# Rotary exchange by DMA issued from ScalarE in the last heads, scaling on ScalarE, and another product order at the ends of the Strassen-like chains

## The chip, the cores and the metric

One Trainium2 chip, one core of it. The metric is the device time of one execution in microseconds; for the kernel before it is the median of three runs. All work is in fp32, and every product is made of three fp32r matmuls on a high and a low part of each operand (hi·hi, hi·lo, lo·hi).

## The reference, cut to what the change touches

One encoder layer over two groups of 512 tokens of width 1024 (prompt and sample), which share all weights. The change touches the rotary part of the queries, the softmax, and the products with w_mo, w_ao and the feed-forward weights:

```python
def rope(x, cos, sin):
    x1, x2 = jnp.split(x, 2, axis=-1)
    return jnp.concatenate([x1 * cos - x2 * sin, x1 * sin + x2 * cos], axis=-1)

# one head of attention (8 heads: 128 plain + 64 rotary query columns, values of 128)
s = q_nope @ k_nope.T + q_rope @ k_rope.T
p = jax.nn.softmax(s * scale, axis=-1)
o = p @ v
# both branches, merge, output, feed-forward
y_m = (sigmoid(o) * hm) @ w_mo
y_a = mla_attention(...) @ w_ao
x = x + (g_m * y_m + g_a * y_a) @ w_out
x = x + (silu(h2 @ w_gate) * (h2 @ w_up)) @ w_down
```

## The kernel before

The stages follow each other on one core: input projections, the mLSTM heads (to about 540 us), the eight attention heads (575 to 859), a first chain of products for w_mo and w_ao (859 to 1020), the output projection, a second chain for the feed-forward weights (about 1150 to 1776), the embedding gate and the last norm. Operands are kept transposed, with channels on the 128 partitions and 512 tokens along the row. Except where a block is pinned, a scheduler sets the order of each engine's instructions from a model of times, and each engine then runs its own list in order; a change of one instruction can so move others.

**Attention.** The loop at L1042 goes over heads `hd` and groups `g`: `attn(hd, g)` (L791) is followed by `attn_proj(hd + 1, g)` (L773), which prepares the next head, and by single steps (`hops`) that prepare the operands of the first chain, a few for each head. `attn_proj` makes the rotated queries in even heads for two heads at a time: the projection `pj` in PSUM, its product with the cosines (L744, `rp`), its product with the sines with neighbouring blocks of 32 rows exchanged (`rs`), and the sum of both (L755), all by `rope` (L741). In every head but head 0 the exchange is made by four multiplications of 32 rows each that write to other rows than they read (L754). In head 0 one multiplication of 128 rows writes `rm` (L748), and four transfers that SyncE issues bring its blocks to their places in `rs` (L752). ScalarE then casts the sum to the high parts `qs` (L778, L779) and VectorE makes the low ones (L780, L781). `attn` goes over four blocks of 128 queries: five matmuls of scores `sc` (L799 to L803), the maximum (L805, L806), the exponential (L808), the reciprocal of the sum (L809), the scaling of the probabilities by it, on ScalarE (L811) and for the block `i == 1` on VectorE (L813), four transposes into `pt` (L816), the high part on ScalarE (`aph`, L818) and the low part on VectorE (`apl`, L154). The value product `av` (L823 to L825) follows with all four blocks; `oz` (L827) is its copy, which goes to memory.

**Chains.** `chain` (L957) makes seven-product (Winograd) block multiplications. An object `Seven` (L904) is one set of four weight blocks, loaded by two transfers of 512 KB issued by ScalarE (L913, `wst`). `weights(name)` (L919) makes the weights of a product, by four adds of 128x512 per set on the engine `adds` (L927 and L928 for P7, L930 for P6, L937 for P3), and splits them (`wp`: L900 on ScalarE, L154 on VectorE). `product` (L941) issues twelve matmuls (L952 to L954) into a PSUM bank. P1 opens bank `b1`, and P6, P5 and P3 add to it; after P1, P6 and P5 ScalarE copies its contents to `u` (L987), so the next product in that bank waits for the copy. `chain` writes the order out:

```python
for n in ("P6", "+P1", "P5", "+P2", "Q4", "+P7", "P3"):   # "+": the next set's
```

The sets of the first chain are mo0 to mo3 and ao0 to ao3; those of the second are the feed-forward ones. `pair` (L1033) picks the engine of the adds in the first chain, VectorE (`V`) or GpSimd (`GP`).

Of the kernel before, what the change touches and what calls it, by code (L numbers as in the profile page):

```python
# [22 lines left out]
AH = 8  # L23
# [39 lines left out]
def encoder_kernel(ctx: ExitStack, tc: tile.TileContext, a):  # L63
    nc = tc.nc
# [324 lines left out]
    for g in range(G):  # L389
        s = EV("ch", "gsb")  # L390
# [349 lines left out]

    def rope(src, nblk, by_dma=False):  # L741
        n = 32 * nblk
        r = Q("tr", "rp")
        V.tensor_tensor(out=r[0:n], in0=src[0:n], in1=cos[0:n], op=ALU.mult)  # L744
        s = Q("tr", "rs")
        m = EV("ch", "rm") if by_dma else None
        if by_dma:
            V.tensor_tensor(out=m, in0=src, in1=sin, op=ALU.mult)  # L748
        for i in range(nblk):
            f, o = slice(32 * i, 32 * i + 32), slice(32 * (i ^ 1), 32 * (i ^ 1) + 32)  # L750
            if by_dma:
                nc.sync.dma_start(s[o], m[f])  # L752
            else:
                V.tensor_tensor(out=s[o], in0=src[f], in1=sin[f], op=ALU.mult)  # L754
        V.tensor_tensor(out=r[0:n], in0=r[0:n], in1=s[0:n], op=ALU.add)  # L755
        return r
# [16 lines left out]
    def attn_proj(hd, g, wa):  # L773
        if hd % 2 == 0:
            r = rope(proj1(wa, lat["cq"][g], 2, 0, "pj"), 4, hd == 0)
            st0 = Q("qst", "qs0", F32R)
# [14 lines left out]
    def attn(hd, g, ops):  # L791
# [4 lines left out]
        for i in range(NB):  # L796
# [12 lines left out]
            V.reciprocal(out=mx[:, 3:4], in_=mx[:, 2:3])  # L809
            if i != 1:  # L810
                S.activation(out=p, in_=p, func=AF.Copy, scale=mx[:, 3:4])  # L811
# [92 lines left out]
    class Seven:  # L904


        def __init__(self, srcs, kh, ops, out, adds=None):
# [8 lines left out]
            self.st, self.n, self.kh, self.ops, self.out = st, n, kh, ops, out  # L916
            self.bk = {}

# [22 lines left out]
        def product(self, name):  # L941
            whi, wlo = self.weights(name)
            b, first = {"P1": ("b1", 1), "P6": ("b1", 0), "P5": ("b1", 0), "P3": ("b1", 0), "P2": ("b0", 1),
# [13 lines left out]
    def chain(quads, head=False, look=4):  # L957

        order = [(0, n) for n in ("P1", "P2", "P7")]
        if head:  # L960
            order = [(0, "P1"), (0, "P2"), (1, "P1"), (1, "P2"), (0, "P7"), (0, "P6"), (0, "P5"), (0, "Q4"), (1, "P7"), (0, "P3")]
        for i in range(1 if head else 0, len(quads)):
            for n in ("P6", "+P1", "P5", "+P2", "Q4", "+P7", "P3"):
                if n[0] != "+":
# [68 lines left out]
    def pair(kind, c, ops, put):  # L1033
        e = V if kind == "mo" and c > 1 or kind == "ao" and c < 2 else GP
        srcs = [a["w8"][W8[f"{kind}{i}"]] for i in (c, c + 4)]
# [485 lines left out]
```

## Time and profile before

| what | value |
|---|---|
| median of three runs | 1883.64 us (1883.53 to 1885.17) |
| the profiled execution | 1885.68 us |
| its span in the trace | 1883.9 us |
| its mean granted TensorE clock | 0.993 |
| TensorE busy | 1844.1 us (98%) |
| VectorE busy | 1233.1 us (65%) |
| ScalarE busy | 884.5 us (47%) |
| GpSimd busy | 350.6 us (19%) |

PE is the matmuls of TensorE, PEld its weight loads, DVE VectorE, ACT ScalarE, POOL GpSimd, SP SyncE; a "q" behind an engine's name is its instruction queue, where transfers are issued. Matmuls overlap, so that one shows 0.39 us and the next starts sooner than that. The engines' shares are means over stages that differ much.

### The profile page before, as it was taken

What the parts mean: (1) busy time and instruction counts of PE and PEld (TensorE: products, weight loads), DVE (VectorE), ACT (ScalarE), POOL (GpSimd) and SP (SyncE); (2) the same over time, 40 slices, a digit from 0 to 9 for tenths busy, and PEclk for the clock granted to TensorE, in tenths of its full rate; (3) what the DMA queues carried; (4) which work ended last, traced back from release to release, by engine and by line L of the source; (5) the groups of instructions that cost most, each with busy time, mean ns of one, the idle gap of its engine ahead of it and who ended that gap; (6) DMA issues with size and microseconds to landing.
All of it is one profiled execution on the core that took longest, in us unless ns stands there. A gap on an engine that the chain in (4) does not pass through costs nothing.

```text
span 1883.9 us, 24465 instructions
## 1 busy us (share of the span) xinstructions
PE 1844.1 (98%) x8849; PEld 1534.2 (81%) x8849; DVE 1233.1 (65%) x2208; ACT 884.5 (47%) x1726; POOL 350.6 (19%) x273
## 2 busy tenths in 40 slices
PE   9999999999999999899999999999999999999997
PEld 7899898988887888677877888888888877878886
DVE  7747575836554667975887487444444569878756
ACT  6255465534444666774534256333333344434433
POOL 0000000100000000250030002666466523111000
PEclk9999999999999999999999999999999999999998
DMA  4111111112254223445555342232323347533332
GB/s 166 52 45 35 57 34 58 40 60 73 79 176 135 65 73 95 125 150 196 164 193 174 101 151 79 95 129 92 103 91 106 119 144 240 159 129 109 99 133 95
DMA packets 98377, 208.11 MB, mean 110 GB/s; under 512 B 10832, under 2 KB 21456, under 8 KB 98256
## 3 DMA queue, kind: packets, MB, share of 16 engines
q1 hardware_dynamic: 85600, 161.72, 25.7%
q10 hardware_dynamic: 12096, 43.00, 7.0%
q8 instruction: 69, 1.13, 0.3%
q0 software_dynamic: 560, 1.84, 0.2%
q14 instruction: 52, 0.43, 0.1%
HBM read 151.89 MB, written 54.10 MB: 109 GB/s over the span
## 4 chain that ended last, share of the span: by engine, by line
PE 85%; DVE 9%; DMA 2%; ACT 2%; issue 1%; SPq 0%; ACTq 0%; DVEq 0%
PE b L952 13%; PE b L954 12%; PE b L953 12%; PE mm L183 8%; PE mm L185 8%; PE mm L184 8%; PE nm L633 3%; PE mm L79 3%; DVE xl L154 2%; PE mm L548 2%; PE mm L550 2%; PE mm L549 2%; PE pt L816 1%; PE mm L1312 1%; PE mm L1313 1%
## 5 line engine op out<-in xcount | busy, mean ns | idle before, releaser
L952 PE MATMUL b<-xh,wp 128*128 128x512 f32 x1148 | 441.8, 393 | 8.9 <-ACT u L987 3.7
L953 PE MATMUL b<-xl,wp 128*128 128x512 f32 x1148 | 448.2, 392 | 0.5 <-DVE xl L154 0.5
L954 PE MATMUL b<-xh,wp 128*128 128x512 f32 x1148 | 444.3, 392 | 0.7 <-DVE wp L154 0.7
L900 ACT CAST wp<-wst 128x512 fp32r<-128x512 f32 (+1 forms) x270 | 164.1, 612 | 306.8 <-PE b L954 256.6
L154 DVE TENSOR_TENSOR wp<-wst,wp 128x512 fp32r<-128x512 f32 (+1 forms) x270 | 233.1, 865 | 72.1 <-ACT wp L900 72.0
L952 PEld LDWEIGHTS b<-xh,wp 128*128 128x128 f32 x1148 | 215.8, 188 | 60.9 <-ACT u L987 7.6
L954 PEld LDWEIGHTS b<-xh,wp 128*128 128x128 f32 x1148 | 216.0, 188 | 48.6 <-DVE wp L154 1.6
L953 PEld LDWEIGHTS b<-xl,wp 128*128 128x128 f32 x1148 | 216.0, 188 | 48.0 <-DVE xl L154 1.4
L183 PE MATMUL mm<-hh,whi 128*128 128x512 f32 x560 | 220.3, 393 | 0.6 <-ACT raw L79 0.3
L184 PE MATMUL mm<-hl,whi 128*128 128x512 f32 x560 | 219.5, 392 | 0.0
L185 PE MATMUL mm<-hh,wlo 128*128 128x512 f32 x560 | 219.3, 392 | 0.0
L992 DVE TENSOR_TENSOR u<-b,u 128x512 f32<-128x512 f32 x90 | 61.6, 689 | 135.2 <-PE b L954 83.7
L183 PEld LDWEIGHTS mm<-hh,whi 128*128 128x128 f32 x560 | 105.6, 189 | 23.2 <-ACT raw L79 0.8
L168 ACT CAST whi<-wst 128x1024 fp32r<-128x1024 f32 (+1 forms) x69 | 71.0, 1029 | 113.7 <-PE mm L184 75.1
L185 PEld LDWEIGHTS mm<-hh,wlo 128*128 128x128 f32 x560 | 105.5, 188 | 21.9
L184 PEld LDWEIGHTS mm<-hl,whi 128*128 128x128 f32 x560 | 105.6, 189 | 21.4
L927 POOL TENSOR_TENSOR s<-wst,wst 128x512 f32<-128x512 f32 (+1 forms) x28 | 43.8, 1565 | 347.3 <-DMA wst<-w 175.1
L154 DVE TENSOR_TENSOR wlo<-wst,whi 128x1024 fp32r<-128x1024 f32 (+1 forms) x69 | 82.2, 1192 | 30.5 <-ACT whi L168 30.0
L987 ACT COPY u<-b 128x512 f32<-128x512 f32 x90 | 50.8, 589 | 108.9 <-PE b L954 85.7
L1210 POOL TENSOR_TENSOR sg<-sg,u 128x512 f32<-128x512 f32 x30 | 54.5, 1818 | 218.0 <-DVE u L992 218.0
L154 DVE TENSOR_TENSOR xl<-ld,xh 128x512 fp32r<-128x512 f32 x121 | 90.2, 773 | 7.2 <-ACT xh L884 6.5
L154 POOL TENSOR_TENSOR vnl<-avt,vnh 128x512 fp32r<-128x512 f32 x16 | 21.2, 1322 | 309.7 <-ACT vnh L158 251.3
(357 smaller groups left out, 3598.5 us busy)
## 6 DMA issues: line engine op xcount, KB each, us to landing
wst<-w SPq DMA_DIRECT2D x73, 512.0 KB
wst<-w ACTq DMA_DIRECT2D x60, 512.0 KB
ld<-actd SPq DMA_DIRECT2D x77, 256.0 KB
actd<-t SPq DMA_DIRECT2D x40, 256.0 KB
x<-x SPq DMA_DIRECT2D x32, 256.0 KB
ld<-hzd SPq DMA_DIRECT2D x32, 256.0 KB
wst<-wd ACTq DMA_DIRECT2D x16, 512.0 KB
actd<-sg SPq DMA_DIRECT2D x30, 256.0 KB
```

The costliest lines, as they stand in the source:

```text
L79: r = f(*args, **kw)
L154: e.tensor_tensor(out=out, in0=src, in1=hi.bitcast(F32), op=ALU.subtract)
L168: S.copy(hi[:, :n], st[:, :n])
L183: E.matmul(bk, whi[:, c], hi, start=k == 0, stop=False)
L184: E.matmul(bk, whi[:, c], lo, start=False, stop=False)
L185: last_mm[0] = E.matmul(bk, wlo[:, c], hi, start=False, stop=k == nk - 1)
L633: E.matmul(bk, l, r, start=n == 0, stop=n == len(terms) - 1)
L900: S.copy(hi, src)
L952: E.matmul(bk, whi[:, c], hi, start=bool(first) and k == 0, stop=False, **sk)
L953: E.matmul(bk, whi[:, c], lo, start=False, stop=False, **sk)
L954: E.matmul(bk, wlo[:, c], hi, start=False, stop=k == self.kh - 1, **sk)
L992: V.tensor_tensor(out=t, in0=b, in1=t, op=ALU.add if name == "P2" else ALU.subtract)
```

## The change

Four edits:

1. In the heads 4 and 6 (two groups each, so four rotations) the exchange of rows goes as in head 0, but the transfers are issued by ScalarE (`S`).
2. The scaling of block `i == 1` goes from VectorE to ScalarE in heads 4, 5 and 6 (six instructions).
3. The last three sets of each chain get orders of their own, and the weights of P7 are made ahead of those of P6 where P7 follows P6.
4. In the first chain the adds of mo2 and ao1 go from VectorE to GpSimd.

```diff
-    def rope(src, nblk, by_dma=False):
+    def rope(src, nblk, by_dma=None):
...
             if by_dma:
-                nc.sync.dma_start(s[o], m[f])
+                by_dma.dma_start(s[o], m[f])
             else:
                 V.tensor_tensor(out=s[o], in0=src[f], in1=sin[f], op=ALU.mult)
...
-            r = rope(proj1(wa, lat["cq"][g], 2, 0, "pj"), 4, hd == 0)
+            r = rope(proj1(wa, lat["cq"][g], 2, 0, "pj"), 4, nc.sync if hd == 0 else S if hd >= 4 else None)
...
-            if i != 1:
+            if i != 1 or 4 <= hd < AH - 1:
                 S.activation(out=p, in_=p, func=AF.Copy, scale=mx[:, 3:4])
...
-            self.bk = {}
+            self.bk, self.w = {}, {}
...
         def product(self, name):
-            whi, wlo = self.weights(name)
+            if name == "P6" and "P7" not in self.w:
+                self.w["P7"] = self.weights("P7")
+            if name not in self.w:
+                self.w[name] = self.weights(name)
+            whi, wlo = self.w[name]
...
+        full = ("P6", "+P1", "P5", "+P2", "Q4", "+P7", "P3")
+        ends = {
+            len(quads) - 3: ("P6", "+P1", "P5", "+P2", "Q4", "P3"),
+            len(quads) - 2: ("P6", "P7", "P5", "+P1", "Q4", "P3"),
+            len(quads) - 1: ("P6", "P7", "P5", "P2", "Q4", "P3"),
+        }
         for i in range(1 if head else 0, len(quads)):
-            for n in ("P6", "+P1", "P5", "+P2", "Q4", "+P7", "P3"):
+            for n in ends.get(i, full):
...
-        e = V if kind == "mo" and c > 1 or kind == "ao" and c < 2 else GP
+        e = V if (kind, c) in (("mo", 3), ("ao", 0)) else GP
```

The scheduler moves other instructions with these. The number of matmuls stays. The three places below are those that matter for what follows; the names carry running numbers.

VectorE before, rotation of head 6, first group: `pj_7778` is the projection, `rp_7785` and `rs_7787` the two parts of the rotation, `pt` and `apl` the transposed probabilities of head 4, second group, and their low part, `xl` low parts of operands of the first chain.

```order
L744 TENSOR_TENSOR rp_7785<-pj_7778,cos 128x512
L754 TENSOR_TENSOR rs_7787<-pj_7778,sin 32x512
L154 TENSOR_TENSOR apl_7532<-pt_7566,aph_7531 128x4x128
L754 TENSOR_TENSOR rs_7787<-pj_7778,sin 32x512 x3
L805 TENSOR_REDUCE mx_7728<-sc_7722 128x1
L809 RECIPROCAL mx_7688<-mx_7688 128x1
L154 TENSOR_TENSOR xl_7839<-ld_7827,xh_7837 128x512
L154 TENSOR_TENSOR apl_7532<-pt_7586,aph_7531 128x4x128
L809 RECIPROCAL mx_7708<-mx_7708 128x1
L154 TENSOR_TENSOR xl_7845<-ld_7841,xh_7843 128x512
L755 TENSOR_TENSOR rp_7785<-rp_7785,rs_7787 128x512
```

VectorE with the change, the same rotation (`rp_7789`, `rs_7791`, and `rm_7792` before its exchange); `pt_7868` to `pt_7928` are the four blocks of head 5, second group.

```order
L748 TENSOR_TENSOR rm_7792<-pj_7782,sin 128x512
L154 TENSOR_TENSOR apl_7854<-pt_7868,aph_7853 128x4x128
L154 TENSOR_TENSOR xl_8304<-ld_8292,xh_8302 128x512
L154 TENSOR_TENSOR apl_7854<-pt_7888,aph_7853 128x4x128
L755 TENSOR_TENSOR rp_7789<-rp_7789,rs_7791 128x512
L154 TENSOR_TENSOR apl_7854<-pt_7908,aph_7853 128x4x128
L154 TENSOR_TENSOR apl_7854<-pt_7928,aph_7853 128x4x128
```

The rotation's product and its sum have moved back: the sum now stands between the low parts of the second and the third block of one value product. In the same place ScalarE has, with the change (`oz` the copy of the value product before, `vnh` and `qnh` casts of projections, `xh` a high part for the first chain):

```order
L818 CAST aph_7853<-pt_7868 128x4x128
L827 COPY oz_7779<-av_7766 128x512
L884 CAST xh_8302<-ld_8292 128x512
L818 CAST aph_7853<-pt_7888 128x4x128
L752 DMA rs_7791<-rm_7792 32x512 x4
L158 CAST vnh_7829<-avt_7827 128x512
L818 CAST aph_7853<-pt_7908 128x4x128
L818 CAST aph_7853<-pt_7928 128x4x128
L158 CAST qnh_7981<-pj_7974 128x512
L778 CAST qs_1320_7799<-rp_7789 64x512
L779 CAST qs_1321_7800<-rp_7789 64x512
```

The four issues stand behind the cast of the second block; the casts of the rotated rows (L778, L779) come after the last block's. What TensorE has between the transposes of the second and of the last block, ahead of the value product `av_7935`:

```order
L816 MATMUL pt_7888<-ident,p_7884 128x128 x4
L799 MATMUL sc_8070<-knh_7823,qnh_7812 128x512
L800 MATMUL sc_8070<-knl_7825,qnh_7812 128x512
L801 MATMUL sc_8070<-knh_7823,qnl_7814 128x512
L183 MATMUL pj_7974<-cqh_5518,whi_7680 128x512
L184 MATMUL pj_7974<-cql_5520,whi_7680 128x512
L185 MATMUL pj_7974<-cqh_5518,wlo_7682 128x512
L183 MATMUL pj_7974<-cqh_5522,whi_7680 128x512
L184 MATMUL pj_7974<-cql_5524,whi_7680 128x512
L185 MATMUL pj_7974<-cqh_5522,wlo_7682 128x512
L816 MATMUL pt_7908<-ident,p_7904 128x128 x4
L816 MATMUL pt_7928<-ident,p_7924 128x128 x4
```

Nine matmuls of 512 columns stand between the second block's transposes and the third's; the value product, which needs all four blocks, follows.

GpSimd before, adds of the first chain (`wst_8644` is of mo1, `wst_9544` and `wst_9546` are of ao2):

```order
L937 TENSOR_TENSOR wst_8644<-wst_8644 128x512
L927 TENSOR_TENSOR s_1743_9653<-wst_9544,wst_9546 128x512
L928 TENSOR_TENSOR wst_9546<-wst_9546 128x512
L930 TENSOR_TENSOR wst_9544<-wst_9544,wst_9546 128x512
L937 TENSOR_TENSOR wst_9544<-wst_9544 128x512
```

GpSimd with the change (`wst_8810` and `wst_8812` of mo2, `wst_9386` and `wst_9388` of ao1; `wst_8652` is mo1 as before):

```order
L937 TENSOR_TENSOR wst_8652<-wst_8652 128x512
L927 TENSOR_TENSOR s_1583_8913<-wst_8810,wst_8812 128x512
L928 TENSOR_TENSOR wst_8812<-wst_8812 128x512
L930 TENSOR_TENSOR wst_8810<-wst_8810,wst_8812 128x512
L937 TENSOR_TENSOR wst_8810<-wst_8810 128x512
L927 TENSOR_TENSOR s_1723_9511<-wst_9386,wst_9388 128x512
L928 TENSOR_TENSOR wst_9388<-wst_9388 128x512
L930 TENSOR_TENSOR wst_9386<-wst_9386,wst_9388 128x512
L937 TENSOR_TENSOR wst_9386<-wst_9386 128x512
L927 TENSOR_TENSOR s_1750_9683<-wst_9552,wst_9554 128x512
```

Eight adds have come in between those of mo1 and of ao2; they left VectorE's list. On TensorE the product of ao2 that opens its bank b1 stands 13 matmuls later in the first chain than before, and in the last set P5 and P3, which add to one bank, still follow each other.

## Rows read from the trace of the kernel before

**Rows 1.** The head of the page: the span, and each engine's busy time with its share of the span.

```profile
span 1883.9 us, 24465 instructions
PE 1844.1 (98%) x8849; PEld 1534.2 (81%) x8849; DVE 1233.1 (65%) x2208; ACT 884.5 (47%) x1726; POOL 350.6 (19%) x273
```

**Rows 2.** The waits of TensorE over the whole program: the waiting operation and its line, the one that ended the wait, total us, times, longest us.

```profile
PE sc L799 <- ACT p L808: 4.6, 5, 2.4
PE b L952 <- ACT u L987: 3.7, 9, 0.7
```

**Rows 3.** Busy time of each engine in stretches of the program: start:end and length in us, then busy us and (number of instructions) of PE, PEld, DVE, ACT and POOL, the granted clock of TensorE as a share of full speed, the busy share of the DMA engines, GB/s.

```profile
718.00:745.00 27.00, 27.00 (x132) 22.24 (x131) 23.73 (x51) 19.03 (x38) 1.29 (x1) 1.00 0.25 77
775.00:800.00 25.00, 20.70 (x100) 16.30 (x100) 24.59 (x48) 20.09 (x42) 5.71 (x5) 1.00 0.36 114
800.00:835.00 35.00, 32.35 (x155) 25.67 (x153) 28.20 (x62) 25.78 (x57) 13.47 (x10) 0.95 0.43 147
835.00:860.00 25.00, 22.15 (x100) 16.59 (x101) 13.12 (x32) 15.70 (x34) 11.48 (x10) 0.93 0.25 90
860.00:925.00 65.00, 65.00 (x286) 53.38 (x285) 46.91 (x75) 29.42 (x54) 1.68 (x1) 1.00 0.61 208
925.00:950.00 25.00, 25.00 (x111) 20.54 (x110) 25.00 (x42) 13.94 (x25) 0.00 (x0) 1.00 0.62 192
```

**Rows 4.** The timeline at the rotation of head 6, first group: start us, duration us, engine, line, operation, out<-in, shape, count, and in brackets the idle time before it and what ended it.

```profile
781.90 0.60 PE L816 MATMUL pt<-ident,p 128*128 128x128 f32 x4
782.03 0.68 DVE L755 TENSOR_TENSOR rp<-rp,rs 128x512 f32<-128x512 f32 x1
782.75 0.62 ACT L778 CAST qs<-rp 64x512 fp32r<-64x512 f32 x1 [1.70 <-DVE rp L755]
784.86 0.50 PE L799 MATMUL sc<-knh,qnh 128*128 128x512 f32 x1 [2.36 <-ACT p L808]
```

**Rows 5.** The timeline at the rotation of head 6, second group, same columns.

```profile
790.41 2.79 DVE L754 TENSOR_TENSOR rs<-pj,sin 32x512 f32<-32x512 f32 x4
792.50 0.50 PE L799 MATMUL sc<-knh,qnh 128*128 128x512 f32 x1 [1.00 <-ACT p L808]
799.68 0.50 PE L183 MATMUL pj<-cqh,whi 128*128 128x512 f32 x1 [0.94 <-DVE qnl L154]
```

**Rows 6.** The timeline of GpSimd, VectorE and TensorE where a scaling of head 6 meets an add on GpSimd, same columns.

```profile
803.90 1.65 POOL L930 TENSOR_TENSOR wst<-wst,wst 128x512 f32<-128x512 f32 x1 [8.44 <-DVE wp L154]
804.35 1.49 DVE L813 TENSOR_SCALAR p<-p,mx 128x512 f32<-128x512 f32 x1
805.75 0.68 DVE L154 TENSOR_TENSOR apl<-pt,aph 128x512 fp32r<-128x512 f32 x1
806.49 0.50 PE L825 MATMUL av<-apl,vnh 128*128 128x512 f32 x1 [1.96 <-DVE apl L154]
```

**Rows 7.** Instructions of single source lines over the whole program: line, engine, operation, count, duration ns (shortest/median/longest), start us of the first and the last, shapes.

```profile
L754 DVE TENSOR_TENSOR rs<-pj,sin x24: 680/686/696, 646.5 to 792.5; 32x512 f32<-32x512 f32 x24
L748 DVE TENSOR_TENSOR rm<-pj,sin x2: 681/682/682, 576.0 to 582.2; 128x512 f32<-128x512 f32 x2
L811 ACT ACTIVATE p<-p,mx x48: 706/726/795, 594.2 to 849.9; 128x512 f32<-128x512 f32 x48
L813 DVE TENSOR_SCALAR p<-p,mx x16: 470/486/1489, 592.5 to 847.6; 128x512 f32<-128x512 f32 x16
L913 ACTq DMA_DIRECT2D wst<-w x60: 334/334/441, 537.0 to 1517.9; - x60
```

**Rows 8.** The timeline at the rotation of head 0, first group, which already goes by transfers: their issues on SyncE's queue, and the sum on VectorE, columns as in the timelines above.

```profile
576.69 2.50 SPq L752 DMA_DIRECT2D rs<-rm  x4
580.79 0.69 DVE L755 TENSOR_TENSOR rp<-rp,rs 128x512 f32<-128x512 f32 x1 [1.07 <-DMA rs<-rm]
```

**Rows 9.** The timeline of VectorE, ScalarE and its queue, and TensorE around the weights of ao2 in the first chain, same columns.

```profile
951.97 0.68 DVE L154 TENSOR_TENSOR wp<-wst,wp 128x512 fp32r<-128x512 f32 x1
953.07 0.33 ACTq L913 DMA_DIRECT2D wst<-w  x1
959.78 0.62 ACT L900 CAST wp<-wst 128x512 fp32r<-128x512 f32 x1 [1.98 <-DMA wst<-w]
960.45 0.50 PE L952 MATMUL b<-xh,wp 128*128 128x512 f32 x1 [3.27 <-ACT wp L900]
```

**Rows 10.** The weight adds as instructions of their source lines over the whole program, columns as for the source lines above.

```profile
L927 POOL TENSOR_TENSOR s<-wst,wst x28: 1017/1300/5170, 755.6 to 1732.7; 128x512 f32<-128x512 f32 x26, 128x384 f32<-128x384 f32 x2
L927 DVE TENSOR_TENSOR s<-wst,wst x14: 558/692/827, 880.5 to 1745.5; 128x512 f32<-128x512 f32 x12, 128x384 f32<-128x384 f32 x2
L930 POOL TENSOR_TENSOR wst<-wst,wst x28: 1212/1624/1737, 803.9 to 1735.1; 128x512 f32<-128x512 f32 x26, 128x384 f32<-128x384 f32 x2
```

**Rows 11.** The timeline of TensorE at the ends of the first and the second chain.

```profile
1012.01 0.50 PE L952 MATMUL b<-xh,wp 128*128 128x512 f32 x1 [0.68 <-ACT u L987]
1015.71 0.50 PE L952 MATMUL b<-xh,wp 128*128 128x512 f32 x1 [0.68 <-ACT u L987]
1772.02 0.47 PE L952 MATMUL b<-xh,wp 128*128 128x512 f32 x1 [0.87 <-DVE x L1248]
```

**Rows 12.** The timeline of TensorE after the stop at 806.49: two like matmuls half a microsecond apart.

```profile
807.29 0.39 PE L825 MATMUL av<-apl,vnh 128*128 128x512 f32 x1
807.86 0.63 PE L824 MATMUL av<-aph,vnl 128*128 128x512 f32 x1
```

## The prediction

> **What bounds the kernel now.** I read the page first: TensorE is busy 1844.1 of 1883.9 us [rows 1], so all that a change can give back is TensorE's 40 us of stops, or clock. The waits of TensorE, by what ended them, come next [rows 2]: the largest entries are scores that wait for an exponential (4.6 us) and products that wait for a copied result (3.7 us). The table of stretches tells where [rows 3]: from 718 to 745 TensorE has no idle time at all, from 775 to 800 it works 20.70 of 25 us while VectorE works 24.59 and ScalarE 20.09, from 925 to 950 it is full again and VectorE too (25.00 of 25.00), and 111 matmuls in 25 us give the pitch of a 512-column matmul, 0.225 us. So head 6 is bound by VectorE, and by ScalarE where it waits for VectorE; the middle of the chain has a full VectorE that TensorE does not wait for, yet. A measurement of this kernel tells about 0.2%, 3.8 us, from no change.
>
> The timeline shows the mechanism in head 6. The rotation's last sum runs on VectorE at 782.03, the cast of it on ScalarE had waited 1.70 us, the exponential stands behind the casts, and TensorE stops 2.36 us for it [rows 4]. In the second group four short multiplications hold VectorE for 2.79 us from 790.41, and TensorE stops 1.00 and then 0.94 us [rows 5]. At 804.35 the scaling on VectorE takes 1.49 us where 0.486 is its median, a GpSimd add running beside it, and the low parts behind it come late: 1.96 us [rows 6, 7]. These four stops are 6.3 us, and they are what the change's first two edits aim at.
>
> **Rotations (heads 4 and 6, two groups each).** Each loses four VectorE rows of 0.686 us and gains one of 0.682 [rows 7]: 2.06 us less for VectorE, 8.2 in all. It gains four transfers issued by ScalarE. Head 0 already works so, from SyncE: from the first issue at 576.69 to the sum at 580.79 are 4.1 us, 2.50 of them the four issues; an issue on ScalarE's queue takes 0.334 [rows 7, 8], 1.3 for four, so the path lies between 2.9 and 4.1 us. The sum now waits for a transfer, and VectorE runs in order, so what stands behind the sum waits too.
> Head 4: nothing. In 718 to 745 TensorE had no stop, VectorE was idle 3.3 us, and the edit lightens VectorE by 4.1 there; the wait of the two sums (two paths less the rows between, 2 × 3.4 = 6.8) is about that cover (7.4). If the path were 2 us longer, it would show.
> Head 6, first group: in the new order the issue stands behind the second block's cast, one VectorE row lies between it and the sum, and behind the sum are two low parts that the value product needs. The path to them is 2.9 to 4.1, up to 0.6 if the issue waits for the cast itself, and three VectorE rows at 0.6 each (1.9): 4.8 to 6.6. TensorE's cover from the second block's transposes on is nine matmuls (2.0), two groups of transposes (0.60 each in the row, about 0.43 net of overlap [rows 4]) and two products of high parts (0.45): 3.3. **New stop 1.5 to 3.3; I take 2.2**, a little under the middle, since the issues will be ScalarE's.
> Head 6, second group: the issue follows the copy of the value product, and the first transposes need a scaling that stands behind the casts of the rotated rows on ScalarE: 0.6 + 4.1 + 0.7 + 2 × 0.62 + 0.73 = 7.4 against 39 matmuls, 8.8 us. Covered by itself, but ScalarE has exponentials, two weight casts and a value cast in that list too, some 7.7 us of work. 0 to 2.5; I take 0.9, nearer the covered end.
>
> **Scaling in heads 4 to 6.** Six VectorE rows of 0.486 (3.9 us with the held one) become six of 0.726 on ScalarE (+4.4 us) [rows 7]. ScalarE had 25.78 busy of 35 from 800 and 19.03 of 27 from 718 [rows 3]; its 4.4 us and 16 issues (5.3) fit by sums there. In head 6 they don't fit freely, which is why the 0.9 above is not nothing.
> So attention: the four stops go (−6.3), 2.2 and 0.9 come: **−3.2 us**. The stops after 835 belong to head 7, which keeps its code: 0.
>
> **Adds of two weight sets.** Those of mo2 fall in 875 to 890, where TensorE never stops and VectorE works 46.91 of 65 us [rows 3]; 0. Those of ao1 go from VectorE (0.692 each) to GpSimd (1.300 each, 1.624 for the third [rows 10]): 5.5 us of GpSimd work in a stretch where VectorE is full. VectorE loses 2.8 us of work. What the row at 804.35 shows is that VectorE is held while GpSimd adds [rows 6]; if each of the four adds holds it for its length, VectorE comes out 2.8 us later, else 2.8 earlier.
> The Trainium skill, page "SBUF — State Buffer", section "Who interferes with whom", states the harder form: a VectorE instruction with two SBUF inputs and a GpSimd one that reads SBUF exclude each other, the later blocks fully until the first ends; this speaks against moving ao1's adds. The trace agrees for the held scaling (1.49 us). By that rule alone the sum would end at −2.9.
>
> **Order of the last three sets.** The stop of 3.27 us at 960.45 waits for a weight cast, this for a load, which was issued at 953.07 when VectorE had split a weight at 951.97, and landed 6.7 us later [rows 9]. In the new order the product that stopped comes 13 matmuls later: 2.9 us more cover, 0.35 left. But P3 of ao0 now starts two matmuls behind the P5 whose bank it adds to, and so waits for a copy: 0.7 at the most in such waits so far [rows 2], for one or two of them. Together −1.8. If the held VectorE issues the load 2.8 us later, it is +1.0 instead. **I take the middle, −0.4.**
> At the chain's end two stops of 0.68 wait for copies; the order keeps P5 and P3 of the last set together, so one remains: **−0.7**. The 0.87 at the end of the second chain keeps its neighbours: 0 [rows 11].
> Clock: after the stop at 806.49 the matmuls go from 0.39 to 0.63 us, the granted clock being at 1.2 instead of 2.4 GHz for 3.4 us [rows 12], 1.7 us lost. The granted clock of 0.95 in 800 to 835 and of 0.93 in 835 to 860 [rows 3] is one such stretch each. I count none gone, since new stops come.
>
> **Sum:** −3.2 − 0.4 − 0.7 = −4.3. Against the profiled execution, 1885.68 (span 1883.9), it gives 1881.4; that one was 2.04 above the median of the three runs, 1883.64, which is what I forecast from: **1879.3**.
>
> **Rivals.**
> *Stops only change their name* (same). In head 6 the sum's wait, in front of the low parts, and the fuller ScalarE take back all 6.3: for it that both engines are full there, against it that VectorE is lightened by 5 of 53 us there [rows 3]. Attention 0, chain +1.0, end −0.7: **1884.0**.
> *VectorE held by GpSimd in the chain.* Each of ao1's four adds holds it as the row at 804.35 shows: load later, stop kept and a wait for copies added; attention as forecast. −3.2 + 1.0 − 0.7 = −2.9: **1880.8**, under what can be measured. This is the case that the page's rule above speaks of.
> *The transfer path is long* (slower). The one load timed here took 6.7 us from issue to use [rows 9], and head 0's rotation ran with no rows of attention behind it. With 6.7 instead of 4.1 the first group of head 6 stops 5.6 us (+3.4), the second +1.2, and in head 4 two sums hold VectorE 6.0 each against a cover of 7.4 (+4.6): +9.2 on the forecast, **1888.5**. It is slower by over 0.2% from a path of 6.4 us on. Against it: a rotation moves 32 rows four times, an eighth of that load each, and head 0's rows say 4.1.
> *All stops vanish*, and with them two stretches of half clock at 1.7 each (that of 800 to 835, and one at the chain's stop): −6.3 + 0.5, −1.8, −1.4, −3.4: −12.4, **1871.2**. For it: the lighter VectorE was the cause of each stop. Against it: the order of the new low parts.
>
> **How the numbers follow.** Forecast 0.40 (its own range, −1.5 to −7 us, lies three quarters beyond 3.8: 0.30 faster, 0.10 same), stops that vanish 0.15 (faster), stops renamed 0.17 (same), held VectorE 0.10 (0.02 faster, 0.08 same), long path 0.18 (slower). Faster 0.47, same 0.35, slower 0.18. The range runs from 1872.5, short of all stops vanishing, to 1887.0, the path's bound halfway to its rival.
>
> **What would show it.** In the new profile: the four stops of head 6 (784 to 807) gone as named; the sum of the rotation waiting for its transfer 1 to 3 us; one wait of a value product for low parts in the first group of head 6; VectorE rows of 1 us and more beside GpSimd's adds near 940 to 955; the wait for a weight cast near 960 under 1 us; one stop of 0.68 at the chain's end. I am wrong if the path from ScalarE is over 6 us, if the scores still wait for exponentials by 4 us in sum, or if the chain's stop grows.

## Result: 0.21% slower, and the profile after

The changed kernel takes 1886.84 us (median of 20 runs, 1884.45 to 1889.39), the kernel before 1883.01 (20 runs beside them, 1880.53 to 1886.21). The ratio is **1.0021, 95% interval 1.0016 to 1.0027**: 3.9 us slower. I had forecast 4.3 us faster, so the sign is wrong.

The head of the profile after shows why shares of busy time say little here: VectorE has 9 us less work than in [rows 1], the span is longer all the same.

```profile
span 1885.0 us, 24492 instructions
PE 1845.2 (98%) x8849; PEld 1534.4 (81%) x8849; DVE 1224.0 (65%) x2182; ACT 888.3 (47%) x1732; POOL 371.1 (20%) x281
```

The waits of TensorE (columns as in [rows 2]):

```profile
PE pj L183 <- DVE knl L154: 3.5, 1, 3.5
PE av L823 <- ACT aph L818: 2.7, 3, 1.2
PE av L825 <- DVE apl L154: 2.4, 1, 2.4
PE b L956 <- ACT u L997: 2.3, 7, 0.7
PE pj L183 <- DVE qnl L154: 2.1, 2, 1.7
PE sc L799 <- ACT p L808: 0.8, 2, 0.6
```

Against [rows 2]: scores wait for exponentials 0.8 us instead of 4.6, as forecast. In their place stand a wait that the kernel before doesn't have, a projection for `knl` (3.5), and more of waits that it has: value products for `aph` (2.7, before 0.7) and for `apl` (2.4, before the 2.0 of [rows 6], which went), a projection for `qnl` (2.1 with 1.7 in one piece, before 1.7 in three). Products wait for copies 2.3 instead of 3.7. The stretches, as in [rows 3], and last the first of them in the kernel before:

```profile
745.00:775.00 30.00, 26.45 (x118) 21.54 (x118) 18.24 (x38) 19.45 (x40) 5.46 (x4) 0.94 0.45 142
775.00:800.00 25.00, 24.32 (x119) 18.61 (x119) 22.40 (x48) 23.07 (x51) 8.71 (x6) 1.00 0.42 125
800.00:835.00 35.00, 29.27 (x133) 22.58 (x132) 24.99 (x53) 24.74 (x52) 10.08 (x7) 0.95 0.39 113
835.00:860.00 25.00, 22.46 (x113) 17.23 (x111) 16.46 (x40) 19.80 (x44) 16.46 (x14) 1.00 0.51 182
925.00:950.00 25.00, 25.00 (x111) 20.54 (x110) 25.00 (x43) 13.23 (x24) 5.88 (x2) 1.00 0.53 168
```

```profile
745.00:775.00 30.00, 28.88 (x136) 22.90 (x135) 22.10 (x48) 20.78 (x43) 8.52 (x7) 1.00 0.46 139
```

775 to 800, the worst stretch before (TensorE 20.70 of 25), is nearly full: 24.32. The loss has moved to both sides of it, 745 to 775 (26.45 against 28.88) and 800 to 835 (29.27 against 32.35). One stretch of half clock now lies in the first of them (0.94); the one that lay in 835 to 860 is gone (1.00 against 0.93). Each of the two traces has four such stretches of 3.4 us ahead of the last stage, two of them in attention, so between these two executions the clock makes no difference.

Adding up TensorE's stops of 0.25 us and more: in attention (from 575 to the first chain) 11.0 us before and 14.3 after; in the first chain 5.4 before and 3.5 after. By its profile, then, the change loses 3.3 us in attention, and what the chain gives back is 1.9. The two profiled executions lie 1.0 us apart by the time they come to attention, and each has its own stretches of half clock; the medians are the measure, the traces the places.

The timeline at the rotation of head 6, first group, shows the mechanism in one place (VectorE, ScalarE and its queue, TensorE; columns as in [rows 4]):

```profile
801.42 0.67 DVE L748 TENSOR_TENSOR rm<-pj,sin 128x512 f32<-128x512 f32 x1
803.44 0.53 ACTq L752 DMA_DIRECT2D rs<-rm  x1
805.94 0.62 ACT L158 CAST vnh<-avt 128x512 fp32r<-128x512 f32 x1 [1.15 <-issue]
807.58 0.50 PE L823 MATMUL av<-aph,vnh 128*128 128x512 f32 x1 [1.24 <-ACT aph L818]
808.73 0.69 DVE L755 TENSOR_TENSOR rp<-rp,rs 128x512 f32<-128x512 f32 x1 [3.10 <-DMA rs<-rm]
809.34 1.28 DVE L154 TENSOR_TENSOR apl<-pt,aph 128x512 fp32r<-128x512 f32 x2
810.68 0.50 PE L825 MATMUL av<-apl,vnh 128*128 128x512 f32 x1 [2.36 <-DVE apl L154]
```

The product `rm` is ready at 802.1. Its first transfer is issued at 803.44, behind the copy `oz` and a cast in ScalarE's list, and the sum runs at 808.73: the path is 5.3 us from the first issue. VectorE, which runs in order, sits idle 3.10 us in front of that sum, and the two low parts `apl` that stand behind it (809.34) are those that the value product waits for: 2.36 us at 810.68. ScalarE has a stop of 1.15 us behind the issues, so the high parts come late as well: 1.24 us at 807.58. Together 3.6 us.

The issues themselves, and who waited for them, by source line (columns as in [rows 7], then us and times):

```profile
L752 ACTq DMA_DIRECT2D rs<-rm x16: 514/602/619, 731.1 to 816.2; - x16
  DVE rp L755: 10.9, 5
```

An issue of these transfers takes ScalarE's queue 0.602 us, not the 0.334 of its weight loads [rows 7]. The sums waited 10.9 us in five waits, one of which (1.1 us) is head 0's: 9.8 us in the four new rotations.

Head 4's two rotations, with their sums' waits and the first stop behind them:

```profile
731.06 0.59 ACTq L752 DMA_DIRECT2D rs<-rm  x1
735.26 0.90 DVE L755 TENSOR_TENSOR rp<-rp,rs 128x512 f32<-128x512 f32 x1 [2.54 <-DMA rs<-rm]
737.43 0.50 PE L823 MATMUL av<-aph,vnh 128*128 128x512 f32 x1 [0.78 <-ACT aph L818]
742.62 2.51 ACTq L752 DMA_DIRECT2D rs<-rm  x4
748.26 0.69 DVE L755 TENSOR_TENSOR rp<-rp,rs 128x512 f32<-128x512 f32 x1 [3.73 <-DMA rs<-rm]
```

The largest new stop, 3.54 us at 768.09, lies behind the second of them:

```profile
742.89 7.59 SPq L787 DMA_DIRECT2D avt<-vd  x3
747.71 0.62 ACT L158 CAST vnh<-avt 128x512 fp32r<-128x512 f32 x1 [5.21 <-DMA rs<-rm]
762.39 4.79 SPq L832 DMA_DIRECT2D ld<-hzd  x3
765.15 1.69 DVE L862 TENSOR_TENSOR ld<-ld,ld 128x512 f32<-128x512 f32 x1 [4.27 <-DMA ld<-hzd]
767.36 0.68 DVE L154 TENSOR_TENSOR knl<-pj,knh 128x512 fp32r<-128x512 f32 x1
768.09 0.80 PE L183 MATMUL pj<-ckvh,whi 128*128 128x512 f32 x1 [3.54 <-DVE knl L154]
```

`avt`, the next head's values, takes the buffer that the rotation's `rs` had. Its load on SyncE so waits for the rotation's transfers and for the sum; three such loads take SyncE's queue from 742.89 to 750.48; in the kernel before three of them were out by 735.7. Loads of the chain's operands (`hzd`) stand behind them and come late, the first at 750.57, before at 742.69. The one that VectorE waits 4.27 us for at 765.15 was issued at 762.39, when a store that had itself come late had left its buffer; `knl` behind it is what the projection needs. ScalarE, too, stands still for 5.21 us ahead of the cast of `avt`, until the rotation's transfers are there.

### The profile page after: what moved, and what is told of

Read it like the earlier page. It is cut to its first block, busy times and chain, and to the rows that moved or that the text cites. A ratio compares the mean times of both kernels' runs of the same rounds, so it can differ in the third digit from the quotient of the medians.

```text
span 1885.0 us, 24492 instructions
## 1 busy us (share of the span) xinstructions
PE 1845.2 (98%) x8849; PEld 1534.4 (81%) x8849; DVE 1224.0 (65%) x2182; ACT 888.3 (47%) x1732; POOL 371.1 (20%) x281
## 4 chain that ended last, share of the span: by engine, by line
PE 85%; DVE 8%; DMA 3%; ACT 2%; issue 2%; ACTq 0%; SPq 0%; DVEq 0%
PE b L956 12%; PE b L958 12%; PE b L957 12%; PE mm L183 8%; PE mm L185 7%; PE mm L184 7%; PE mm L79 3%; PE nm L633 3%; PE mm L548 2%; PE mm L550 2%; PE mm L549 2%; DVE xl L154 1%; PE mm L1323 1%; PE mm L1322 1%; PE mm L1321 1%
```

## Experiments

All are compared with runs of the kernel before on the same chip; a difference in us is the ratio less 1, times 1883.

| kernel | edits in it | ratio to before (95%) | us |
|---|---|---|---|
| the change | rotations, scaling, order, adds | 1.0021 (1.0016 to 1.0027) | +3.9 |
| e1 | rotations alone | 1.0056 (1.0043 to 1.0068) | +10.5 |
| e2 | all but the rotations | 0.9985 (0.9974 to 0.9995) | −2.8 |
| e3 | order and adds | 0.9990 (0.9981 to 0.9999) | −1.9 |
| e4 | scaling alone | 0.9987 (0.9978 to 0.9996) | −2.4 |
| e5 | the change, transfers from SyncE | 0.9998 (0.9988 to 1.0008) | −0.4 |
| e6 | the change, transfers in head 4 only | 0.9998 (0.9987 to 1.0009) | −0.4 |
| e7 | the change, transfers in head 6 only | 0.9999 (0.9986 to 1.0013) | −0.2 |
| e8 | the change, `avt` loaded from GpSimd | 1.0031 (1.0016 to 1.0046) | +5.8 |
| e9 | e5, idle issues on ScalarE | 0.9992 (0.9982 to 1.0002) | −1.5 |
| e10 | the change, transfers from GpSimd | 1.0008 (0.9997 to 1.0019) | +1.5 |
| e11 | the change, transfers in head 2 instead | 1.0001 (0.9992 to 1.0009) | +0.2 |
| e12 | scaling and order | 0.9981 (0.9972 to 0.9991) | −3.6 |
| e13 | the change, sum behind the low parts | 1.0002 (0.9989 to 1.0014) | +0.4 |
| e14 | e13 with transfers from SyncE | 0.9976 (0.9964 to 0.9989) | −4.5 |
| e15 | the change without the exchange | 0.9972 (0.9960 to 0.9984) | −5.3 |

One caution holds for all: the scheduler lays out the order anew for each kernel (dozens to hundreds of TensorE's 8849 rows stand in another place from one to the next), so a single stop may move for reasons beside the edit. I read the ratios first, and traces for where.

### Which edit costs it: e1 to e4

e1, edits 2 to 4 undone:

```diff
-            if i != 1 or 4 <= hd < AH - 1:
+            if i != 1:
...
-        ends = {
...
+        ends = {}
...
-        e = V if (kind, c) in (("mo", 3), ("ao", 0)) else GP
+        e = V if kind == "mo" and c > 1 or kind == "ao" and c < 2 else GP
```

> The kernel before with edit 1 alone (rotations of heads 4 and 6 by transfers issued from ScalarE). Theory R (the rotations cost it: an issue holds ScalarE about 0.6 us and the sum waits 3 us for its transfer in front of other VectorE work): +3 to +5 us against before, with TensorE stops of 2 to 4 us behind the sum in heads 4 to 6. Theory S (scaling on ScalarE makes it too full): within 1 us of before. Theory P (adds on GpSimd hold VectorE in the chain): within 1 us or faster.

e2, edit 1 undone:

```diff
-            r = rope(proj1(wa, lat["cq"][g], 2, 0, "pj"), 4, nc.sync if hd == 0 else S if hd >= 4 else None)
+            r = rope(proj1(wa, lat["cq"][g], 2, 0, "pj"), 4, nc.sync if hd == 0 else None)
```

> The changed kernel without edit 1 (rotations of heads 4 and 6 as before, the other three edits in). Theory R: faster than before, by 1 to 4 us, since the stop of 3.27 us in the chain shrinks and nothing is lost in attention. Theory S and theory P: +3 to +5 us, as the whole change.

e3 has edit 1 undone as in e2 and the scaling as in e1; e4 has edit 1, the order and the adds undone.

> The kernel before with the edits of the chains alone (order of the last three sets, adds of mo2 and ao1 on GpSimd). Theory R: 1 to 3 us faster than before, attention unchanged to 0.3 us. Theory P: the stop near 960 stays at 3 us or grows, 0 to +2 us.

> The kernel before with edit 2 alone (six scalings of heads 4 to 6 on ScalarE). Theory R: within 1.5 us of before; the held scaling and its stop of 1.96 us near 806 go. Theory S: +2 us or more, with scores waiting for exponentials in head 6.

Measured: +10.5, −2.8, −1.9, −2.4 us. The rotations are the whole loss, and alone they cost more than theory R had (3 to 5). The stops don't show that more: in attention they sum to 14.0 us in e1's profile, 14.3 in the change's. The clock shows a part. The mean granted clock over all runs is 0.9910 in e1 and 0.9937 in the kernel before beside it, and over the runs of the kernel before alone the time falls by 1.5 to 1.8 us for each 0.001 of it; so I estimate that 4 to 5 of the 10.5 us are stretches at 1.2 instead of 2.4 GHz. In e2 to e4 the mean is 0.9947 to 0.9950, which by the same estimate is about 2 us of what each gains. The scaling alone and the order with the adds gain; theories S and P fall. In e2 head 6 still has a stop behind the four short multiplications, and one behind `qnl`, but the two others of [rows 4, 6] are gone:

```profile
791.64 0.50 PE L183 MATMUL pj<-cqh,whi 128*128 128x512 f32 x1 [1.91 <-DVE rs L754]
798.91 0.50 PE L183 MATMUL pj<-cqh,whi 128*128 128x512 f32 x1 [1.06 <-DVE qnl L154]
```

So a part of what I had credited to the rotations comes with the other edits, the scaling among them.

### Who issues, and where in the program: e5 to e8

e5, e6 and e7 change one expression, the issuer:

```diff
-nc.sync if hd == 0 else S if hd >= 4 else None
+nc.sync if hd in (0, 4, 6) else None               # e5
+nc.sync if hd == 0 else S if hd == 4 else None     # e6
+nc.sync if hd == 0 else S if hd == 6 else None     # e7
```

> The changed kernel with the transfers of heads 4 and 6 issued from SyncE, as head 0 does, instead of ScalarE. Theory I (each issue holds ScalarE 0.6 us, 2.4 us a rotation, and the casts behind it come late): 2 us or more faster than the change, so at or under before; ScalarE shows no idle time behind issues. Theory W (VectorE waits in order for transfers, whoever issues): within 1.5 us of the change, +2 to +5 on before. Theory Q (SyncE's queue is held by a load that waits for the rotation's buffer, and the loads of the chain's operands behind it come late): as the change or slower, since the issues then stand in that queue too.

> The changed kernel with transfers in head 4 alone (head 6 multiplies as before). Theory Q: the stop of 3.5 us near 768 belongs to head 4's second rotation and stays; about +3 us against the change without rotations by transfer (which was -2.8 on before), so about 0 to +1 on before. Theories I and W, which charge each rotation alike: half of the 6.7 us that the four rotations cost, +0.5 on before, but as stops of 1 to 2 us behind the casts and sums near 735 and 748, not near 768.

> The changed kernel with transfers in head 6 alone. Theory W: the stops near 807 to 811 (3.6 us) and near 823 to 827 (2.1 us) stay, and no stop of over 1 us near 768; 2 to 4 us slower than without any of them, so -1 to +1 on before. Theory Q: head 6 costs under 1 us net, so about -2 on before.

e8 takes the load that waits for the rotation's buffer out of SyncE's queue:

```diff
-        nc.sync.dma_start(vt.rearrange("p (a b) -> p a b", a=NB), vd[g][hd // 4].rearrange("a p c -> p a c")[:, :, c : c + P])
+        nc.gpsimd.dma_start(vt.rearrange("p (a b) -> p a b", a=NB), vd[g][hd // 4].rearrange("a p c -> p a c")[:, :, c : c + P])
```

> The changed kernel with the attention values loaded by transfers issued from GpSimd instead of SyncE, so that a load that waits for the rotation's buffer no longer stands ahead of the loads of the chain's operands in SyncE's queue. Theory Q: the stop of 3.5 us near 768 goes and the operand loads start before 745 again; 2 to 4 us faster than the change, about at before. Theories I and W: within 1.5 us of the change, the stop near 768 stays or moves.

Measured: −0.4, −0.4, −0.2 and +5.8 us. Issuing from SyncE takes back 4.3 of the change's 3.9 + 2.8; sums then wait 2.6 us for transfers in heads 4 and 6, not 9.8. Heads 4 and 6 cost about the same by the medians, 2.4 and 2.6 us on e2 (the four rotations together 6.7), which speaks against theory Q (head 4's load chain as the main part); e7's interval, −2.6 to +2.4, doesn't exclude the −2 that theory Q gave it. e8 speaks against it more clearly: the stop for `knl` shrinks to 0.5 us, and other stops take its place (waits of TensorE, columns as in [rows 2]):

```profile
PE sc L802 <- DVE qs L780: 2.7, 1, 2.7
PE av L823 <- ACT aph L818: 5.1, 4, 1.8
PE pj L183 <- DVE knl L154: 0.5, 1, 0.5
```

Theory Q named a real stop but not the cost: when that one is taken away, TensorE waits elsewhere, for low parts of the rotated rows and for ScalarE's high parts, while the sums still wait for their transfers, and the total is no better.

### The issues, or the late transfers: e9 and e10

```diff
             by_dma.dma_start(s[o], m[f])          # e9: SyncE in heads 4 and 6
+            if dummy:                             # in heads 4 and 6
+                S.dma_start(scr[o], m[f])         # scr: scratch in memory
```

> The changed kernel with the four rotations' transfers issued from SyncE (which was 4 us faster than the change), and beside each of them one more transfer of the same rows, issued from ScalarE into a scratch buffer in memory that nothing reads. ScalarE so has the 16 issues of the change at nearly the same places of its list, but no sum waits for them. Theory I1 (what costs is ScalarE's time in the issues): 2 to 4 us slower than with SyncE alone, +2 to +4 on before. Theory I2 (what costs is that the real transfers start late, behind other rows of ScalarE's list, so that VectorE waits for them): within 1 us of the SyncE version, about at before, though ScalarE shows the same idle time behind issues as in the change.

Measured: −1.5 us, against −0.4 without the idle issues: they cost nothing that this can measure. ScalarE shows stops behind issues as in the change, here 1.70 us in front of `aph`:

```profile
796.42 0.93 ACTq L756 DMA_DIRECT2D scr<-rm  x2
798.37 1.18 ACT L822 CAST aph<-pt 128x512 fp32r<-128x512 f32 x2 [1.70 <-DMA scr<-rm]
```

An idle issue took 0.43 us, not 0.60, so this is not quite the same load on ScalarE; but theory I1 asked for 2 to 4 us and there is none. That leaves the transfers that come late and are waited for.

e10 has `nc.gpsimd` for `S`:

> The changed kernel with the transfers of heads 4 and 6 issued from GpSimd, which has little else in attention. Theory I2: the transfers start as soon as the product is there; the sums wait less than the 9.8 us of the change, and it is 2 to 5 us faster than the change. Theory W (the path itself, not the issuer): within 1.5 us of the change. If the path from GpSimd is longer than from SyncE, between them.

Measured: +1.5 us (interval across no change), by the medians 2.4 faster than the change and 1.9 slower than from SyncE; its interval touches both of theirs. The sums waited 2.2 us in it, head 0's included. So the issuer matters by how soon it comes to the issue, as I2 has it; whether GpSimd gains less than SyncE, and why, I leave open.

### Does a looser stretch cover it: e11

`nc.sync if hd == 0 else S if hd == 2 else None`: two rotations in head 2, none in heads 4 and 6.

> The changed kernel with transfers issued from ScalarE in head 2 instead of heads 4 and 6. TensorE has no stops in head 2 of the kernel before, and VectorE and ScalarE work about 60% there. Theory C (the price depends on how full VectorE and ScalarE are around it): within 1 us of the version without such rotations, -2 to -3 us on before, though its sums wait 2 to 4 us each. Theory W (each rotation costs what its transfer takes): about +3 us on that version, at before.

Measured: +0.2 us, that is 3.0 on e2. Theory C, which was also my reason for costing head 4 at nothing, falls. The same picture as in head 6, in a place where TensorE had no stop at all and VectorE worked 12.87 of 20 us (660 to 680 in the kernel before):

```profile
663.83 1.89 ACTq L752 DMA_DIRECT2D rs<-rm  x3
665.76 0.62 ACT L158 CAST vnh<-avt 128x512 fp32r<-128x512 f32 x1 [1.72 <-issue]
667.37 0.89 DVE L755 TENSOR_TENSOR rp<-rp,rs 128x512 f32<-128x512 f32 x1 [2.61 <-DMA rs<-rm]
667.40 0.50 PE L823 MATMUL av<-aph,vnh 128*128 128x512 f32 x1 [1.34 <-ACT aph L818]
668.18 1.28 DVE L154 TENSOR_TENSOR apl<-pt,aph 128x512 fp32r<-128x512 f32 x2
669.52 0.50 PE L825 MATMUL av<-apl,vnh 128*128 128x512 f32 x1 [1.38 <-DVE apl L154]
```

The sum waits 2.61 us, the two low parts stand behind it, the high parts behind the issues: 1.34 and 1.38 us of stops. An idle share of VectorE around it is no cover, because these instructions form one chain that ends in a value product.

### The adds: e12

e12 has the edit of e2 and the line of `pair` as in e1.

> The changed kernel without the transfers and without the move of eight adds to GpSimd: scaling on ScalarE and the new order of the last sets only. If adds on GpSimd hold VectorE (theory P), the two stops near 955 (1.5 and 1.2 us with the adds on GpSimd) shrink, and it is 1 to 2 us faster than with them, -4 to -5 on before. If the moved adds help, the stops grow and it is 1 to 2 us slower than with them, -1 on before.

Measured: −3.6 against −2.8 with the adds moved: the same within the intervals, which are about 2 us to either side. In the chain the stops are 0.74, 1.92 and 0.68 us without, 1.50, 1.19 and 0.68 with the moved adds. No effect of the adds shows in either direction; the 1 us that I had put at the low end isn't excluded.

### Where the sum stands: e13 to e15

e13 keeps the issues on ScalarE and queues the sum behind the last low part of the block beside it (`last[0]`, kept by `attn`); the casts follow it:

```diff
+    def finish():                    # called ahead of the next attn_proj, and of attn in even heads
+        while pending:
+            r, s, st0, st1 = pending.pop(0)
+            with tc.issue_after(last[0].ins):
+                V.tensor_tensor(out=r, in0=r, in1=s, op=ALU.add)
+            S.copy(st0[0:64], r[0:64])
...
-            lo_of(pl[:, :, c], tp3, ph[:, :, c])
+            last[0] = lo_of(pl[:, :, c], tp3, ph[:, :, c])
```

> The changed kernel, transfers issued from ScalarE at the same places of its list, but each rotation's sum queued on VectorE behind the last low part (apl) of the attention block that runs beside it; nothing else of the order is set. Theory O (what costs is that the waiting sum stands in front of low parts that TensorE's value product needs): the stops of value products behind VectorE near 737 and 811 go, and it is 2 to 4 us faster than the change, 0 to +2 on before. Theory L (the rotated rows themselves come too late, wherever the sum stands): the stops move to the scores that need the rotated rows, within 1 us of the change, +3 to +5 on before.

Measured: +0.4 us, 3.6 less than the change. The waits of VectorE for the exchanged rows in these rotations fall from 9.8 to 0.8 us, and no value product waits for `apl` any more. From the sum's source line (us, times):

```profile
  DMA rs<-rm: 0.8, 1
```

The edit leaves the transfers and their issuer alone; the sum now stands where it has other work ahead of it. Theory O holds, theory L falls: the rotated rows were not needed as early as the sum was placed. The largest entry left is on ScalarE's side, value products that wait for `aph` (from the waits of TensorE; 0.7 in the kernel before):

```profile
PE av L846 <- ACT aph L841: 4.8, 4, 2.2
```

e14 is e13 with the issuer of e5.

> As the last one, with the transfers issued from SyncE. Theory O: with the sum out of the way and the transfers started early the rotations cost less than with SyncE alone, 1 to 2 us faster than that version, -1 to -3 on before; if the lighter VectorE is worth anything, as fast as the version without such rotations or faster (-3 to -4). Theory L: as with SyncE alone, 0 on before.

Measured: **−4.5 us, faster than both kernels** (0.9976, interval 0.9964 to 0.9989), and no sum in heads 4 and 6 waits for a transfer in its profile. Against e2 it is 1.7 us faster, with intervals that overlap. It is more than theory O had (−1 to −4). What it gains on e13, 4.9 us, can't be the sums' wait, which was 0.8 us there. In e13's profile the cast of `avt` still waits 3.6 us for the rotation's transfers, and the mean granted clock is 0.9942, against 0.9960 in e14 (by the estimate above some 3 us); which of these makes the difference stays open.

e15 leaves the exchange out (the rotated queries of heads 4 to 7 are not those of the reference) and shows what free transfers would be worth:

```diff
+        if by_dma is S:
+            V.tensor_tensor(out=s, in0=src, in1=sin, op=ALU.mult)
+            V.tensor_tensor(out=r[0:n], in0=r[0:n], in1=s[0:n], op=ALU.add)
+            return r
```

> The changed kernel with the exchange of rows left out in heads 4 and 6: one multiplication of 128 rows and the sum, no transfers and no short multiplications (the rotated queries of heads 4 to 7 are so not those of the reference). It shows what the lighter VectorE is worth with transfers that cost nothing. As the prediction had it (the stops of head 6 come from VectorE's four short rows): 3 to 5 us faster than the version without such rotations, -6 to -8 on before. If VectorE's time in the rotations bounds nothing: within 1.5 us of that version, -2 to -4 on before, and then there was nothing for the transfers to gain.

Measured: −5.3 us, 2.5 on e2. The stops of e2 shown above shrink, to 0.79 us and 0.31 us near the same places:

```profile
797.11 0.50 PE L183 MATMUL pj<-cqh,whi 128*128 128x512 f32 x1 [0.79 <-DVE mx L810]
801.85 0.50 PE L829 MATMUL av<-apl,vnh 128*128 128x512 f32 x1 [0.31 <-DVE apl L154]
```

That lies between the two cases that I had set down, 3 to 5 us on e2 or at most 1.5. So the lighter VectorE was worth something, as the prediction had it, but some 2.5 us, less than I had put on it; by the medians e14 gets 1.7 of that, which the intervals don't separate from all or nothing.

## Why the prediction was wrong, point by point

- **The four stops of head 6 go (−6.3).** They went: none of [rows 4 to 6] is in the profile after, and scores wait for exponentials 0.8 us in sum; but one like that for `qnl` at 799.68 comes up one projection later, at 827.30. But only a part needed the rotations. The scaling alone gives 2.4 us (e4), and without any exchange it is 5.3 with all edits (e15).
- **The path of 2.9 to 4.1 us.** Mis-sized: from the first issue to the sum it took 4.2 (731.06 to 735.26) to 5.6 us (742.62 to 748.26). I had put ScalarE's issue at 0.334 us, the row of its weight loads. It was 0.602, what SyncE's own row for the same transfer showed (2.50 for four in [rows 8]); the kind of transfer was the better guide than the engine.
- **Head 4: nothing.** This is the step that failed. It set the sum's waits (6.8) against VectorE's spare time (7.4). They waited 2.54 and 3.73 us, near that, but what stood behind them was on TensorE's path: 0.78 us at 737.43, and 3.54 at 768.09 by way of SyncE's queue. Alone, head 4's rotations cost 2.4 us on e2 (e6). e11 shows that the reasoning was wrong and not the size: in head 2, where VectorE had over a third of its time free, two rotations cost 3.0 us too. Spare time in a stretch does not cover a wait that stands in front of a needed instruction.
- **Head 6, first group: 2.2 (1.5 to 3.3).** Right in mechanism and place, too small: 1.24 + 2.36 = 3.6 us. The path (5.3 instead of at most 4.1) is most of the difference: the same sum with 5.3 gives 3.9.
- **Head 6, second group: 0.9 (0 to 2.5).** 0.45 + 1.68 = 2.1 us, within its bounds, but by luck. The transposes didn't stop for a scaling on ScalarE. What stopped were scores for `qs` (0.45) and a projection for `qnl`, which on VectorE stood behind a low part of 1.67 us where 0.69 is usual, a GpSimd add beside it:

```profile
823.54 1.67 DVE L781 TENSOR_TENSOR qs<-rp,qs 64x512 fp32r<-64x512 f32 x1
827.30 0.50 PE L183 MATMUL pj<-cqh,whi 128*128 128x512 f32 x1 [1.68 <-DVE qnl L154]
```

- **Scaling on ScalarE: no term of its own.** It fits, and it gains 2.4 us (e4), some of it in the clock.
- **Order and adds: −0.4 and −0.7.** The first chain's stops went from 5.4 to 3.5 us, and e3 is 1.9 us faster. In e12 moving the adds back changes nothing that can be measured, so the gain is put down to the order, and the rival of a held VectorE isn't borne out.
- **Clock: nothing.** It fits for the change: attention has two stretches of half clock before and after, and the mean granted clock is 0.9934 over its runs, 0.9937 over the later runs of the kernel before. In the trace of the change the two begin at 767.6 and 812.0, in or just behind its two largest stops (768.09 and 810.68); in e14's, whose longest stop in attention is 1.31 us, there is none. So a stop of 2 us and more can cost its length and, as an estimate, 1.7 us besides (half of the 3.4); the prediction counted this in one rival only.
- **The rivals.** "Stops renamed" described the mechanism (the sum in front of the low parts) but bounded it by what had been gained, which it need not be. "The path is long" had the right sign from a path of 6.4 us on; the time came at 4.2 to 5.6 us, because its sum still used head 4's cover of 7.4 us. In the chances, 3.2 of the 5.5 us from −1.5 to −7 lie beyond 3.8, which is less than the three quarters that I gave.
- **The signs.** None of the three that were to show me wrong appeared: the path stayed under 6 us, scores wait 0.8 us for exponentials, and the chain's stop of 3.27 became two of 1.57 and 1.22. They watched the terms of the sum, and the largest part of the loss came where the sum had put nothing.

In numbers, attention: −6.3 as forecast, +4.3 in head 4 instead of 0, +3.6 instead of 2.2, +2.1 instead of 0.9, so +3.7 in place of −3.2 (the stops in the trace differ by +3.3). With the chain at −1.9 this would be some +1.8; the medians say +3.9, and the traces of single executions, 1 us or two apart by themselves, don't settle the rest; some 0.5 of it would be the clock, by its means. e1, e2, e5, e13 and e14 are what shows the cause: without the rotations the loss is gone, the later placing of the sum takes back 3.6 us, the earlier issue 4.3, both together 8.4. How much of that is the stops themselves and how much the clock isn't separated: its mean rises from 0.9934 in the change to 0.9942 (e13), 0.9953 (e5) and 0.9960 (e14), by the estimate above 1, 3 and 4 to 5 us.

## What to carry to other kernels

Here a transfer replaced arithmetic, and the arithmetic saved was the small term; the engine that waits for the transfer in order, and what stands behind the waiting instruction, was the large one. So issue the transfer from a queue that comes to it at once, and place the instruction that waits behind whatever else is needed first: here that turned +3.9 us into −4.5. A price for an issue is taken from a row of the same kind of transfer, and spare time of an engine is no cover unless it lies between the issue and the first instruction that is needed. And a gain of a few microseconds is read beside the mean granted clock of the runs, since stops and stretches at the lower clock come together.

## What the runs showed of the hardware

VectorE and GpSimd in the chain, with the adds of ao1 on GpSimd (timeline of the changed kernel, then the chain's stops):

```profile
945.56 8.94 POOL L928 TENSOR_TENSOR wst<-wst 128x512 f32<-128x512 f32 x1
954.58 1.63 POOL L930 TENSOR_TENSOR wst<-wst,wst 128x512 f32<-128x512 f32 x1
954.97 1.78 DVE L154 TENSOR_TENSOR wp<-wst,wp 128x512 fp32r<-128x512 f32 x1
956.68 1.77 DVE L871 TENSOR_TENSOR t<-t,ld 128x512 f32<-128x512 f32 x1
959.67 0.50 PE L956 MATMUL b<-xh,wp 128*128 128x512 f32 x1 [1.57 <-DVE xl L154]
964.37 0.50 PE L956 MATMUL b<-xh,wp 128*128 128x512 f32 x1 [1.22 <-ACT wp L900]
1017.07 0.50 PE L956 MATMUL b<-xh,wp 128*128 128x512 f32 x1 [0.68 <-ACT u L997]
```

I had expected GpSimd's adds to hold VectorE for their length. Mostly the reverse happened: the add at 945.56 took 8.94 us where such adds take 1.3, while VectorE ran two-input instructions back to back (25.00 of 25 us busy from 925). Only as it came through did VectorE's rows grow, to 1.78 and 1.77 us beside the next add, some 2.7 us in all with the one ahead. The Trainium skill, page "SBUF — State Buffer", section "Who interferes with whom", has an exclusive lock on the port pair that the two share, and the one that comes later blocked. The rows agree that one of the two stands still; here it was GpSimd, for the length of thirteen VectorE instructions in a row. It cost TensorE nothing that e12 could measure. The held scaling of [rows 6], which I had put beside this, reads one tile and a column of scalars, so it isn't a case of two tiles read.

A second one: a transfer of 32 rows within the on-chip memory occupies the issuing queue 0.60 us (ScalarE) or 0.59 (SyncE), one into memory 0.43 (e9), a 512 KB load 0.33 [rows 7], all by their medians.
